# One 512-column value projection in the first head of a hybrid decoder layer

## Chip, cores and metric

The kernel runs on one core of one Trainium2 chip. The metric is the device time of one execution in microseconds (us). The engines are TensorE (PE, with its weight loads listed as PEld), VectorE (DVE), ScalarE (ACT), GpSimd (POOL) and SyncE (SP), whose queue issues nearly all DMAs.

## What is computed

The reference is one decoder layer on 2048 tokens of width 1024, all in float32. Cut to what matters here:

```python
u = rmsnorm(h, norm_mix_w[l])
proj = u @ w_in[l]
hq, hf, hi, hg, att = jnp.split(proj, [...], axis=-1)
...
v_hg = hi.reshape(B, S, HG_HEADS, HG_DV)           # 4 heads of 128 values
o_hg = hgrn2_chunkwise(q_hg, k_hg, v_hg, log_f)    # recurrence, one state per head
o_hg = rmsnorm(o_hg, hg_norm_w[l]) * silu(hg)
...
mix = jnp.concatenate([o_hg, o_att], axis=-1)
h = h + mix @ w_out[l]
```

The recurrence of a head is S_t = diag(f_t) S_{t-1} + k_t v_t^T with the output o_t = S_t^T q_t, where f comes from hf through a sigmoid and k = 1 - f. Beside it stands an attention of 8 query heads over a window of 128 keys. A gated feed-forward part with a short convolution follows, and a last norm.

## The kernel before

**Tiling.** The tokens are worked on in two halves of 1024 (`for hf in range(NH)`). Each half passes through a mixing stage (projections, recurrence, attention), then `out_proj`, `gate_up` and `down`. Every matrix product is made of three: each operand is split into a high part and the rest (`hi`, `lo`; `XH`, `XL`), and hi x hi, hi x lo and lo x hi are added up in PSUM.

**The mixing stage.** It runs over four heads h, and each holds one recurrence head (`hgrn`) and two of the eight query heads (`attend`). Both are generators, and the loop at the end of the listing says in which order their parts are emitted. A head has four units of 128 output columns by 1024 tokens (`unit`, L197): f, hq, q (the attention's query) and g (the gate). A unit is 48 matmuls whose stationary operand is a weight tile and whose moving operand is 512 tokens. The values are made otherwise: in `project_v` the tokens are stationary and the weights move, so that the result has tokens on its partitions. One call makes two heads. For each of 8 tiles of 128 tokens it runs 8 x 3 matmuls of 256 columns (L566 to L568) and two evacuations on ScalarE (L570). It is called in heads 0 and 2.

**The recurrence of a head.** K and Q are made from f and q (L431, L433). Then come a diagonal product `pdiag` (L441), seven levels (`plev`, L467 and L480, with K and Q scaled by VectorE between them), transposes of K (`pkn`, L506), the state updates (`pu`, L513, which read the values), the output products (`po`, L531 and L532, which read the values too), and a norm and transposes back (L540 to L546). K and Q have one buffer each, and the PSUM tiles of this chain two. For the last head the gate unit is emitted ahead of the levels.

**Buffers.** Weights are fetched and split by `prep`: a DMA on SP's queue into a raw ring of three, a cast on ScalarE (L178) and a subtraction on VectorE (L179), into a ring of two pairs `hi`, `lo`. With `slots` set, the pair goes into two of eight slots of 1024 columns instead (tag "m"). These slots are the homes of the mixing results: one for each of the heads' recurrence and attention outputs (`slot`), in use from the head that makes them until `out_proj`. At the end of a half they hold the residual stream, and `finish` writes it out from them (L971). The values have two buffers of one head each (`VB = 2`).

**Order.** A planner fixes the order of each engine's instructions ahead of time: in a simulated timeline an engine takes, of the instructions that are ready, the one that comes first in program order. On the chip each engine then follows its list, and waits where an operand is late. In program order a head's value projection stands behind its levels and its q unit, and ahead of its attention scores (`psc`, L356), its `pkn` and `pu` and its gate unit.

Of the kernel before, what the change touches and what calls it, by code (L numbers as in the profile page):

```python
# [8 lines left out]
F32 = mybir.dt.float32  # L9
# [3 lines left out]
AF = mybir.ActivationFunctionType  # L13
# [4 lines left out]
P = 128  # L18
D = 1024
KT = D // P  # L20
# [3 lines left out]
TT = HALF // P  # L24
NB = HALF // 512
HG = 4
# [12 lines left out]
NEG = -1.0e30  # L39
UT = 7  # L40
RAW = 3
VB = 2


@with_exitstack
def hymba_layer(ctx: ExitStack, tc: tile.TileContext, a: dict, out: bass.AP):
    nc = tc.nc

    def pool(name, bufs=1, space=None, stack=ctx, **kw):
        if space is not None:  # L50
            kw["space"] = space
        return stack.enter_context(tc.tile_pool(name=name, bufs=bufs, **kw))
# [12 lines left out]
    def ps(kind, name):  # L65
        return spaces[kind].tile([P, 512], F32, tag=kind, name=name)
# [98 lines left out]
    def raw4(src):  # L165
        t = wp.tile([P, D], F32, tag="raw", name="raw", bufs=RAW)
        if src is not None:
            nc.sync.dma_start(t, src)
        return t

    def prep(src, slots=False, parts=(slice(0, D),)):

        raw = raw4(None)
        hi, lo = [hp.tile([P, D], F32R, tag="m", name=f"w{t}", bufs=KT) if slots else
                  wp.tile([P, D], F32R, tag=t, name=f"w{t}", bufs=2) for t in ("hi", "lo")]
        for c in parts:
            nc.sync.dma_start(raw[:, c], src[:, c])
            nc.scalar.copy(hi[:, c], raw[:, c])  # L178
            nc.vector.tensor_tensor(lo[:, c], raw[:, c], hi[:, c].bitcast(F32), op=ALU.subtract)  # L179
        return hi, lo  # L180
# [23 lines left out]
    def split(src, w=None, eng=None, dst=None):  # L204

        h, l = dst or new_x()
        if w is None:
            nc.scalar.copy(h, src)
            (eng or nc.vector).tensor_tensor(l, src, h.bitcast(F32), op=ALU.subtract)  # L209
        else:  # L210
            nc.scalar.activation(h, src, AF.Identity, scale=w)
            nc.vector.scalar_tensor_tensor(l, src, w, h.bitcast(F32), op0=ALU.mult, op1=ALU.subtract)
        return h, l
# [338 lines left out]
        nc.vector.tensor_copy(state[:, h], SS[:, TT - 1])  # L552
        yield

    def project_v(hf, pr, X, rs, p):

        v = [p.tile([P, TT, P], F32, tag="v", name="v", bufs=VB) for _ in range(2)]
        parts = [prep(a["w_v"][pr, s]) for s in range(2)]
        for tt in range(TT):
            o = ps("mm", "pvv")  # L560
            t = slice(tt * P, (tt + 1) * P)
            for kt in range(KT):
                hi, lo = parts[kt // 4]
                xh, xl = X[kt]
                c = slice((kt % 4) * 256, (kt % 4 + 1) * 256)
                nc.tensor.matmul(o[:, 0:256], xh[:, t], hi[:, c], start=kt == 0, stop=False)  # L566
                nc.tensor.matmul(o[:, 0:256], xl[:, t], hi[:, c], start=False, stop=False)  # L567
                nc.tensor.matmul(o[:, 0:256], xh[:, t], lo[:, c], start=False, stop=kt == KT - 1)  # L568
            for i in range(2):
                nc.scalar.activation(v[i][:, tt], o[:, i * P:(i + 1) * P], AF.Identity, scale=rs[:, tt:tt + 1])  # L570
        return v

    def split_into(h, l, src, eng=None):
        nc.scalar.copy(h, src)  # L574
# [398 lines left out]
    X, W = [], []  # L973
# [7 lines left out]
    for hf in range(NH):  # L981
        X, kv, invb, rs, f0 = nxt
        with ExitStack() as st:
            p = pool(f"mix{hf}", stack=st, reuse_waits="tile")
            KS, V = att_keys(hf, kv, invb, p)
            mix = [None] * KT
            vs = []
            M, WG = {}, {}
            for h in range(HG):
                hg = hgrn(hf, h, X, invb, vs, WG, mix, p, f0 if h == 0 else None)  # L990
                at = attend(hf, h, X, invb, KS, V, mix, p)
                next(hg)
                if h == HG - 1:
                    next(at)
                    next(hg)
                    for kt in (0, 4, 1, 5, 2, 6):
                        M[kt] = split(mix[kt])
                    next(hg)
                else:
                    next(hg)  # L1000
                    next(at)
                if h % 2 == 0:
                    vs += project_v(hf, h // 2, X, rs, p)
                if h < HG - 1:
                    WG[h] = prep(a["w_g"][h])
                next(at)
                next(hg)
                if h < HG - 1:
                    next(hg)
                next(at)  # L1010
                if h < HG - 1:
                    next(at)
                    next(hg)
                else:
                    next(hg)
                    next(at)
            M[7], M[3] = mix[7], mix[3]
        with ExitStack() as st:
            p = pool(f"ffn{hf}", stack=st, reuse_waits="tile")
            kept, ops, hs, first = out_proj(hf, M, p)  # L1020
            acts = gate_up(hf, ops, hs, first, p)
            nxt = down(hf, kept, acts, p)


def _layout(i):

    import numpy as np

    def cols(w, idx):
        t = w[:, idx].reshape(KT, P, len(idx))  # L1030
        return t.transpose(1, 0, 2).reshape(P, -1)

    x = i["x"][0]
    w_in = i["w_in"][0]
    ar = np.arange
    att0 = 2048
    att = [np.concatenate([att0 + j * HD + ar(HD), att0 + (j + 4) * HD + ar(HD)]) for j in range(4)]
    att += [att0 + 512 + ar(P), att0 + 640 + ar(P)]
    b = i["b_attn"][0]
    rows = [ar(P) + h * P for h in range(4)]  # L1040
    rows += [512 + np.concatenate([j * HD + ar(HD), (j + 4) * HD + ar(HD)]) for j in range(4)]
    w_out = i["w_out"][0][np.concatenate(rows)]
    w_v = np.stack([cols(w_in, 1024 + pr * 256 + ar(256)).reshape(P, 2, D).transpose(1, 0, 2) for pr in range(2)])
    conv = np.concatenate([i["conv_w"][0], i["conv_b"]], 0)
    d = {
        "xT": x.T.reshape(KT, P, S),
        "xP": x[np.where(ar(S) // 512 % 2, ar(S) ^ 31, ar(S))].T.reshape(KT, P, S),
        "norm_mix_w": i["norm_mix_w"][0].reshape(KT, P).T,
        "w_q": np.stack([cols(w_in, h * P + ar(P)) for h in range(4)]),
        "w_f": np.stack([cols(w_in, 512 + h * P + ar(P)) for h in range(4)]),  # L1050
        "w_v": w_v,
        "w_g": np.stack([cols(w_in, 1536 + h * P + ar(P)) for h in range(4)]),
        "w_att": np.stack([cols(w_in, c) for c in att]),
        "b_attn": np.stack([b[c - att0] for c in att], 1),
        "lb_logits": i["lb_logits"].reshape(2, HG, P).transpose(2, 0, 1),
        "hg_norm_w": i["hg_norm_w"].reshape(P, 1),
        "sinks": i["sinks"].reshape(2, 4).T.reshape(1, 8),
        "w_out": np.stack([cols(w_out, t * P + ar(P)) for t in range(KT)]),
        "norm_ffn_w": i["norm_ffn_w"].reshape(KT, P).T,
        "final_norm_w": i["final_norm_w"].reshape(KT, P).T,  # L1060
        "w_gate": np.stack([cols(i["w_gate"][0], t * P + ar(P)) for t in range(FT)]),
        "w_up": np.stack([cols(i["w_up"][0], t * P + ar(P)) for t in range(FT)]),
        "conv": conv.reshape(4, FT, P).transpose(2, 1, 0),
    }

    w = i["w_down"][0].reshape(FT // 2, 2, P, 2, 4, P)
    d["w_down"] = w.transpose(3, 1, 2, 0, 4, 5).reshape(4, P, FT // 2, 512)
    return {k: np.ascontiguousarray(v) for k, v in d.items()}
# [16 lines left out]
```

## Time and profile before

| | |
|---|---|
| median of 3 runs | 2219.83 us (2214.84 to 2221.45) |
| the profiled execution | 2216.09 us, span 2214.4 us |
| granted TensorE clock, mean | 0.996 |
| TensorE busy | 2173.3 us (98%), 11302 matmuls |
| weight loads busy | 1818.8 us (82%) |
| VectorE busy | 1637.8 us (74%) |
| ScalarE busy | 1047.8 us (47%) |
| value projections | 768 matmuls of 256 columns, 64 evacuations |

Busy time is the union of an engine's instructions. Matmuls overlap in the pipeline, so the time from one start to the next, not the duration, is what a matmul costs. The slices of the page cut the span in 40 equal parts; a digit is the busy share in tenths. In the timeline a row gives the start, the length, the engine, the line, the operation, the tiles written and read, the shapes and a count.

### The profile page before, as it was taken

The page shows a single profiled execution, that of the slowest core. Times are in us where ns is not written, and L with a number is a line of the kernel's source. Part 1 is how long each engine was busy: PE and PEld are TensorE (multiplying, and loading weights), DVE is VectorE, ACT ScalarE, POOL GpSimd, SP SyncE. Part 2 cuts the span into 40 slices and gives each one's busy share as a digit, 9 for nine tenths or more (in the row PEclk, how much of TensorE's full clock was granted, in tenths as well). Part 3 has the DMA queues.
Part 4 walks back from the last instruction along what each step waited for, and adds up shares of the span by engine and source line. Part 5 has one row for each costly group of instructions (what it writes and reads, how often), then busy time and mean ns, then how long its engine had stood idle before and what let it go on. Part 6 is the DMA issues. An engine that isn't in the chain of part 4 may idle for free.

```text
span 2214.4 us, 29214 instructions
## 1 busy us (share of the span) xinstructions
PE 2173.3 (98%) x11302; PEld 1818.8 (82%) x11302; DVE 1637.8 (74%) x2458; ACT 1047.8 (47%) x1821; POOL 13.0 (1%) x37
## 2 busy tenths in 40 slices
PE   8999998999999999999999999989999999999997
PEld 6988987778888888888889889878788888888887
DVE  6567568688887888775865666577878888887766
ACT  6445445454444445335725455545544444443353
POOL 2000000000000000000000000000000000000000
PEclk9999999999999999999999999999999999999998
DMA  4111112322333234964631111213232323359643
GB/s 154 39 29 39 29 39 67 107 84 92 113 100 114 88 127 146 372 233 160 201 124 39 29 29 39 67 29 132 66 126 85 124 87 119 96 196 388 223 130 128
DMA packets 89995, 254.15 MB, mean 115 GB/s; under 512 B 11008, under 2 KB 13184, under 8 KB 89856
## 3 DMA queue, kind: packets, MB, share of 16 engines
q1 hardware_dynamic: 87552, 251.17, 33.8%
q8 instruction: 88, 1.44, 0.3%
q10 hardware_dynamic: 2304, 1.12, 0.2%
q14 instruction: 51, 0.42, 0.1%
HBM read 195.10 MB, written 57.15 MB: 114 GB/s over the span
## 4 chain that ended last, share of the span: by engine, by line
PE 94%; DVE 3%; ACT 1%; DMA 1%; issue 0%; SPq 0%; DVEq 0%; ACTq 0%
PE X L697 7%; PE X L698 7%; PE X L699 7%; PE pop L197 6%; PE hq L197 4%; PE f L197 4%; PE q L197 4%; PE g L197 4%; PE pdx L879 4%; PE pdx L880 4%; PE pdx L881 4%; PE Y L697 4%; PE Y L699 4%; PE Y L698 4%; PE pdy L880 3%; PE pdy L879 3%
## 5 line engine op out<-in xcount | busy, mean ns | idle before, releaser
L574 ACT CAST whi<-raw 128x1024 fp32r<-128x1024 f32 x88 | 92.7, 1053 | 109.3 <-PE X L698 66.8
L698 PE MATMUL X<-T,whi 128*128 128x512 f32 x352 | 137.3, 390 | 0.0
L697 PE MATMUL X<-T,whi 128*128 128x512 f32 x352 | 137.0, 389 | 0.0
L699 PE MATMUL X<-T,wlo 128*128 128x512 f32 x352 | 136.9, 389 | 0.0
L763 DVE SCALAR_TENSOR_TENSOR y<-ga,cw,y 128x1024 f32<-128x1024 f32 x88 | 112.5, 1279 | 28.1 <-ACT y L761 28.1
L703 ACT COPY u<-X 128x512 f32<-128x512 f32 x88 | 51.6, 587 | 121.6 <-PE X L699 121.3
L575 DVE TENSOR_TENSOR wlo<-raw,whi 128x1024 fp32r<-128x1024 f32 x88 | 107.2, 1218 | 0.0
L575 DVE TENSOR_TENSOR xld<-raw,xhd 128x1024 fp32r<-128x1024 f32 x72 | 80.8, 1132 | 18.9 <-ACT xhd L574 18.6
L178 ACT CAST whi<-raw 128x1024 fp32r<-128x1024 f32 (+2 forms) x61 | 63.0, 1035 | 62.0 <-PE hq L197 12.4
L574 ACT CAST xhd<-raw 128x1024 fp32r<-128x1024 f32 x72 | 69.6, 978 | 43.2 <-DMA raw<-act0T 14.7
L197 PE MATMUL pop<-XL,whi 128*128 128x512 f32 x256 | 84.8, 395 | 3.5 <-DVE XL L209 3.5
L197 PE MATMUL pop<-XH,wlo 128*128 128x512 f32 x256 | 83.8, 393 | 0.8 <-DVE wlo L179 0.8
L197 PE MATMUL pop<-XH,whi 128*128 128x512 f32 x256 | 84.1, 400 | 0.2
L179 DVE TENSOR_TENSOR wlo<-raw,whi 128x1024 fp32r<-128x1024 f32 (+2 forms) x61 | 73.2, 1204 | 13.2 <-ACT whi L178 13.2
L697 PEld LDWEIGHTS X<-T,whi 128*128 128x128 f32 x352 | 66.1, 188 | 14.0 <-ACT u L703 0.3
L699 PEld LDWEIGHTS X<-T,wlo 128*128 128x128 f32 x352 | 66.1, 188 | 13.9 <-issue 0.2
L698 PEld LDWEIGHTS X<-T,whi 128*128 128x128 f32 x352 | 66.1, 188 | 13.9 <-issue 0.2
L879 PE MATMUL pdx<-xhd,hid 128*128 128x512 f32 x192 | 74.5, 391 | 1.0 <-ACT hid L574 1.0
L880 PE MATMUL pdx<-xld,hid 128*128 128x512 f32 x192 | 74.8, 390 | 0.0
L697 PE MATMUL X<-T,Sh 128*128 128x512 f32 x176 | 68.7, 390 | 5.3 <-ACT s L703 5.3
L881 PE MATMUL pdx<-xhd,lod 128*128 128x512 f32 x192 | 73.7, 389 | 0.0
L567 PE MATMUL pvv<-whi,XL 128*128 128x256 f32 x256 | 73.1, 287 | 0.0
(359 smaller groups left out, 6530.8 us busy)
## 6 DMA issues: line engine op xcount, KB each, us to landing
wr<-in_w_down SPq DMA_DIRECT2D x90, 512.0 KB, 5.6
raw<-in_w_gate SPq DMA_DIRECT2D x44, 512.0 KB, 3.7
raw<-in_w_up SPq DMA_DIRECT2D x44, 512.0 KB, 3.6
raw<-act0T SPq DMA_DIRECT2D x20, 512.0 KB, 5.9
raw<-act1T SPq DMA_DIRECT2D x20, 512.0 KB, 5.6
act0B<-y SPq DMA_DIRECT2D x33, 256.0 KB, 2.3
act1B<-y SPq DMA_DIRECT2D x33, 256.0 KB, 2.5
raw<-in_w_out SPq DMA_DIRECT2D x16, 512.0 KB, 4.0
```

What stands on the lines that cost most here:

```text
L179: nc.vector.tensor_tensor(lo[:, c], raw[:, c], hi[:, c].bitcast(F32), op=ALU.subtract)
L197: nc.tensor.matmul(o[b], w, x[:, bs], start=f, stop=l)
L567: nc.tensor.matmul(o[:, 0:256], xl[:, t], hi[:, c], start=False, stop=False)
L574: nc.scalar.copy(h, src)
L575: (eng or nc.vector).tensor_tensor(l, src, h.bitcast(F32), op=ALU.subtract)
L697: nc.tensor.matmul(o, wh[:, ws], xh, start=i == 0 and not more, stop=False, skip_group_check=more)
L698: nc.tensor.matmul(o, wh[:, ws], xl, start=False, stop=False, skip_group_check=more)
L699: nc.tensor.matmul(o, wl[:, ws], xh, start=False, stop=i == 3, skip_group_check=more)
L763: nc.vector.scalar_tensor_tensor(y, g[:, w:w + HALF], C.cw[:, ft, w:w + 1], y, op0=ALU.mult, op1=ALU.add)
L879: nc.tensor.matmul(o, wh[:, i, c], ah[:, i, cols], start=f, stop=False, skip_group_check=more)
L880: nc.tensor.matmul(o, wh[:, i, c], al[:, i, cols], start=False, stop=False, skip_group_check=more)
L881: nc.tensor.matmul(o, wl[:, i, c], ah[:, i, cols], start=False, stop=l, skip_group_check=more)
```

## The change

The values of all four heads come from one call, in head 0. A matmul now moves 512 columns, and the 8 x 3 matmuls of a token tile fill a whole PSUM bank. The weights are four pieces of two contraction tiles each. The first goes into the ring, the three others into six of the result slots, which are free in head 0 apart from two. One evacuation per token tile writes all four heads. The values have one buffer for the whole half.

```diff
-VB = 2
...
-    def project_v(hf, pr, X, rs, p):
-
-        v = [p.tile([P, TT, P], F32, tag="v", name="v", bufs=VB) for _ in range(2)]
-        parts = [prep(a["w_v"][pr, s]) for s in range(2)]
+    def project_v(X, rs, p):
+
+        v = p.tile([P, HG, TT, P], F32, tag="v", name="v", bufs=1)
+        parts = [prep(a["w_v"][s], s > 0) for s in range(4)]
         for tt in range(TT):
             o = ps("mm", "pvv")
             t = slice(tt * P, (tt + 1) * P)
             for kt in range(KT):
-                hi, lo = parts[kt // 4]
+                hi, lo = parts[kt // 2]
                 xh, xl = X[kt]
-                c = slice((kt % 4) * 256, (kt % 4 + 1) * 256)
-                nc.tensor.matmul(o[:, 0:256], xh[:, t], hi[:, c], start=kt == 0, stop=False)
-                nc.tensor.matmul(o[:, 0:256], xl[:, t], hi[:, c], start=False, stop=False)
-                nc.tensor.matmul(o[:, 0:256], xh[:, t], lo[:, c], start=False, stop=kt == KT - 1)
-            for i in range(2):
-                nc.scalar.activation(v[i][:, tt], o[:, i * P:(i + 1) * P], AF.Identity, scale=rs[:, tt:tt + 1])
-        return v
+                c = slice(kt % 2 * 512, (kt % 2 + 1) * 512)
+                nc.tensor.matmul(o, xh[:, t], hi[:, c], start=kt == 0, stop=False)
+                nc.tensor.matmul(o, xl[:, t], hi[:, c], start=False, stop=False)
+                nc.tensor.matmul(o, xh[:, t], lo[:, c], start=False, stop=kt == KT - 1)
+            nc.scalar.activation(v[:, :, tt], o.rearrange("p (h d) -> p h d", h=HG), AF.Identity, scale=rs[:, tt:tt + 1])
+        return [v[:, h] for h in range(HG)]
...
-                if h % 2 == 0:
-                    vs += project_v(hf, h // 2, X, rs, p)
+                if h == 0:
+                    vs += project_v(X, rs, p)
...
-    w_v = np.stack([cols(w_in, 1024 + pr * 256 + ar(256)).reshape(P, 2, D).transpose(1, 0, 2) for pr in range(2)])
+    w_v = cols(w_in, 1024 + ar(512)).reshape(P, 4, D).transpose(1, 0, 2)
```

## The prediction

> **What bounds the kernel now.** I read the page first, for the engines and the slices.
>
> ```profile
> span 2214.4 us, 29214 instructions
> ...
> PE 2173.3 (98%) x11302; PEld 1818.8 (82%) x11302; DVE 1637.8 (74%) x2458; ACT 1047.8 (47%) x1821; POOL 13.0 (1%) x37
> ...
> PE   8999998999999999999999999989999999999997
> ...
> PEclk9999999999999999999999999999999999999998
> ```
>
> TensorE is busy 98% of the span at a full clock nearly everywhere, so work taken off TensorE shortens the kernel wherever nothing else is late. The changed work lies in the mixing stage: about 33 to 393 us for the first half of the tokens, 1130 to 1488 us for the second. Next I asked for windows, all instructions in stretches of 10 us (columns: PE busy, PEld, DVE, ACT, POOL, granted clock, DMA).
>
> ```profile
> 80.00:90.00 10.00, 10.00 (x87) 10.00 (x86) 3.36 (x6) 2.57 (x9) 0.00 (x0) 1.00 0.00 0
> 90.00:100.00 10.00, 10.00 (x117) 9.62 (x116) 2.59 (x4) 4.03 (x10) 0.00 (x0) 1.00 0.01 2
> ...
> 220.00:230.00 10.00, 10.00 (x71) 8.03 (x70) 0.00 (x0) 1.80 (x9) 0.00 (x0) 1.00 0.01 2
> ...
> 310.00:320.00 10.00, 10.00 (x75) 8.44 (x74) 1.85 (x3) 2.23 (x10) 0.00 (x0) 1.00 0.19 55
> ...
> 350.00:360.00 10.00, 6.46 (x34) 4.73 (x34) 10.00 (x18) 3.71 (x8) 0.00 (x0) 0.97 0.35 105
> 360.00:370.00 10.00, 9.32 (x34) 7.89 (x35) 7.37 (x17) 7.48 (x35) 0.00 (x0) 0.69 0.01 2
> ```
>
> ```profile
> 340.00:400.00 60.00, 53.39 (x376) 45.06 (x375) 43.42 (x88) 25.97 (x80) 0.00 (x0) 0.94 0.13 38
> 1436.00:1496.00 60.00, 52.47 (x383) 43.75 (x382) 42.63 (x88) 26.14 (x80) 0.00 (x0) 1.00 0.13 37
> ```
>
> Two regimes are to be seen. Up to 340 us TensorE has no idle time and VectorE waits for it; between 350 and 360 us VectorE is full and TensorE waits. This is the tail of head 3, where TensorE has run out of units that don't need head 3's recurrence. The two tails cost 60 - 53.39 = 6.6 us and 60 - 52.47 = 7.5 us of idle TensorE. The waits of that stretch name the recurrence:
>
> ```profile
> PE plev L467 <- ACT G L465: 1.9, 1, 1.9
> PE pop L197 <- DVE XL L209: 1.8, 1, 1.8
> ```
>
> Last came the timeline of TensorE (start, length, instruction), for where the recurrence stands beside the units.
>
> ```profile
> 156.33 0.83 PE L441 MATMUL pdiag<-hg,K 128*128 128x128 f32 x6
> 229.70 0.61 PE L197 MATMUL q<-XH,wlo 128*128 128x512 f32 x2
> 234.69 0.39 PE L532 MATMUL po<-SS,Q 128*128 128x128 f32 x2
> 246.44 1.73 PE L441 MATMUL pdiag<-hg,K 128*128 128x128 f32 x14
> 306.15 0.39 PE L531 MATMUL po<-v,ST 128*128 128x128 f32 x2
> 324.50 0.39 PE L532 MATMUL po<-SS,Q 128*128 128x128 f32 x2
> 335.62 0.62 PE L197 MATMUL g<-XH,wlo 128*128 128x512 f32 x2
> 344.31 1.95 PE L441 MATMUL pdiag<-hg,K 128*128 128x128 f32 x16
> 386.91 0.38 PE L531 MATMUL po<-v,ST 128*128 128x128 f32 x2
> 392.32 0.39 PE L532 MATMUL po<-SS,Q 128*128 128x128 f32 x2
> ```
>
> A head's recurrence opens with its diagonal product (L441) and closes with its output products (L531, L532): 156.3 to 235.1 for head 1, 246.4 to 324.9 for head 2, 344.3 to 392.7 for head 3. The next head's Q has one buffer and must wait for the close. So the recurrence of the four heads is a second, serial chain, and after its last close come only units whose number is fixed. The half ends when the later of the two is through: TensorE's units or this chain.
>
> **The change, part by part.** *Matmuls.* Starts, not durations, tell the cost, since durations overlap.
>
> ```profile
> 91.04 0.28 PE L568 MATMUL pvv<-wlo,XH 128*128 128x256 f32 x1
> ...
> 94.63 0.28 PE L568 MATMUL pvv<-wlo,XH 128*128 128x256 f32 x1
> ```
>
> ```profile
> 703.02 0.39 PE L697 MATMUL X<-T,whi 128*128 128x512 f32 x1
> ...
> 707.78 0.39 PE L697 MATMUL X<-T,Sh 128*128 128x512 f32 x1
> ```
>
> Thirty steps of 256 columns take 3.59 us, 0.1197 us each; twenty-one steps of 512 columns, with new stationary weights at each, take 4.76 us, 0.2267 us each. The change removes 4 stages x 192 = 768 of the first (91.9 us) and adds 2 x 192 = 384 of the second (87.1 us): **-4.8 us**, 2.4 per half. The Trainium skill, in "TensorE: Matmul & The Clock Gate", section "Back-to-back issue gap", gives N/2.4 + 2.5 ns, hence by estimate 109.2 and 215.8 ns, and the sum would be only -1.0 us; the trace's steps are 10 to 11 ns longer, so I go by the rows.
>
> *Evacuations.* 64 copies of 128 columns become 32 of 512.
>
> ```profile
> L570 ACT ACTIVATE v<-pvv,y 128x128 f32<-128x128 f32 x32 | 10.0, 363 | 20.9 <-PE pvv L568 20.8
> L333 ACT ACTIVATE att<-att,bq 128x512 f32<-128x512 f32 x8 | 5.5, 717 | 1.7 <-DVE att L331 1.7
> ...
> L703 ACT COPY u<-X 128x512 f32<-128x512 f32 x88 | 51.6, 587 | 121.6 <-PE X L699 121.3
> ```
>
> Bounded by the last two rows the new one takes 587 to 717 ns: 18.8 to 22.9 us in place of 64 x 363 = 23.2. ScalarE is 47% busy and a token tile now lasts 24 x 0.2267 = 5.4 us against 0.7 to evacuate it; four PSUM banks cover that. Nothing.
>
> *Weight pieces.* Four per half before and after, but two move from head 2 to head 0 with their DMAs on SP's queue, two casts and two subtractions (here over 18 such).
>
> ```profile
> L179 DVE TENSOR_TENSOR wlo<-raw,whi 128x1024 fp32r<-128x1024 f32 x18 | 21.9, 1216 | 4.5 <-ACT whi L178 4.5
> ...
> 1166.30:1195.00 28.70, 24.39 (x192) 23.35 (x192) 4.38 (x14) 1.00 0.06 19
> ...
> 1128.01 4.55 SPq L971 DMA_DIRECT2D out<-h  x8
> ```
>
> That is 2.4 us of VectorE in head 0, hidden by the long projection. In the second half three pieces need six result slots, whose last contents leave by 1132.6 us; the projection lay between 1166.3 and 1195.0 (the row of its own instructions above), which leaves 34 us. In return the second ring slot is free for the next weights. If a piece came late, planned work of later heads would fill in; up to 2 us, taken as nothing.
>
> *The move.* In head 0 the projection grows from 192 x 0.1197 = 23.0 us to 192 x 0.2267 = 43.5, and in head 2 the 23.0 us vanish. Program order puts the scores of a head and its recurrence updates behind the projection, so in head 0 VectorE, at 3.36 and 2.59 of 10 us above, stays that idle for 20.5 us more, and everything through the start of head 2's recurrence comes 20.5 us later. TensorE loses nothing by that. But behind head 2's q unit, which ended at 230.2, TensorE had 336.1 - 230.2 = 105.9 us of work before it ran dry, and now has 82.9, while the chain has the same steps: 324.9 - 230.2 = 94.7 us to the close of head 2, then 67.8 us to the close of head 3. If the chain kept its pace, both closes would come 20.5 us late in each half: the upper bound. If it gained all of it, the half would gain 2.4 us.
>
> It will gain much. The output products of head 2 took 306.15 to 324.9 = 18.7 us, in four batches with q units between; those of head 3, with no units left to put between, took 386.9 to 392.7 = 5.8. With the units used up by 82.9 us, head 2 closes in the same way: **12.9 us back**. Head 2's scores no longer stand behind a projection, and can use stretches such as 220 to 230 us, where VectorE did nothing; some of head 3's attention moves ahead of the tail too. Bounds are 0 and the 10 us of that stretch; I take 3, nearer to 0, since the rest of this stage has VectorE full for short spells only. So per half 20.5 - 12.9 - 3 = 4.6 us later, **about +9 us** in all; the matmul gain is inside this, since the chain sets the end. The profiled execution took 2216.1 us (span 2214.4), 3.7 under the median of 2219.8: 2225 in its terms, 2229 beside the median.
>
> **The rivals.** *The chain follows TensorE* (not slower): VectorE had 10 and 8.2 idle us at 220 and 310; if it uses 10 of these rather than 3 in each half, the chain keeps step with the shorter TensorE work (20.5 - 12.9 - 10 = -2.4 per half), and the -4.8 us show: 2215. It decides at the point where head 3's diagonal product comes no more than 8.2 us behind the end of the last g unit, as 344.3 behind 336.1 now. For it: VectorE waited for TensorE all the way to 340. Against: full VectorE from 350.
>
> *The tail shrinks as well*: attention of head 3 done ahead of the tail takes half of the 14.1 idle us with it: -4.8 - 7 = -12, 2208.
>
> *No pace is gained*: the planner keeps head 2's batches apart, and both closes come 20.5 us late: +41 us, 2261. Against it are the 5.8 us of head 3. The granted clock fell to 0.69 behind the idle stretch in the rows above. The same page of the Trainium skill, section "Why this matters for your kernels", warns of TensorE gaps over about 3 us, after which the clock halves; the 0.69 agrees, and this would add to a longer tail.
>
> *The matmuls don't get cheaper*: at 2 x 0.1197 a step the gain is nothing; the 512-column row with new weights at each step speaks against it.
>
> **How the numbers follow.** The forecast, 2229 with 2226 to 2235 as its own range (VectorE's share of the catch-up between 4.3 and 0 us per half), gets 0.40; the chain following, 2213 to 2226, 0.29; the shrinking tail 0.19; no pace gained, with what lies between it and the forecast, 0.12. About 0.3%, 6.7 us, is what a measurement of this kernel can tell from no change. So faster 0.19, same 0.29, slower 0.52. The range runs from 2207, which cuts off a part of the shrinking tail, to 2248, which cuts off most of the last case.
>
> **What would show it.** Right: 512-column steps of 0.227 us in one stage of some 49 us per half; head 1's diagonal product near 177 us; head 2's output products within 10 us; head 3's close at about 397 and the idle time of 340 to 400 grown by some 7 us. Wrong: head 3's close before 392, or VectorE busy over 60% while the projection runs; steps of 0.24 would undo the first term, and a TensorE wait on a weight piece the third.

## The result, and the profile after

The changed kernel took 2232.87 us (median of 4 runs, 2228.82 to 2235.33) beside 2220.22 us (2214.84 to 2221.45) for the kernel before: a ratio of 1.0058 with a 95% interval of 1.0047 to 1.007, so slower by over 0.3%. The profiled execution took 2228.82 us, its span 12.7 us longer than before.

The page of the changed kernel, in the parts shown of before:

```profile
span 2227.1 us, 28404 instructions
...
PE 2173.5 (98%) x10918; PEld 1802.1 (81%) x10918; DVE 1634.4 (73%) x2458; ACT 1036.7 (47%) x1771; POOL 14.1 (1%) x37
...
PE   8999997999999999999999999989999999999997
```

There are 384 matmuls fewer, but TensorE's busy time is the same, and the seventh slice (334 to 390 us) has gone from 8 to 7: there the loss shows. The timeline of TensorE in the changed kernel (start, length, instruction) gives the same marks as before; its line numbers are one or two lower:

```profile
82.98 0.39 PE L565 MATMUL pvv<-whi,XH 128*128 128x512 f32 x1
...
85.70 0.39 PE L565 MATMUL pvv<-whi,XH 128*128 128x512 f32 x1
...
176.42 0.38 PE L440 MATMUL pdiag<-hg,K 128*128 128x128 f32 x2
...
271.91 0.38 PE L440 MATMUL pdiag<-hg,K 128*128 128x128 f32 x2
...
335.50 0.27 PE L530 MATMUL po<-v,ST 128*128 128x128 f32 x1
...
343.45 0.39 PE L531 MATMUL po<-SS,Q 128*128 128x128 f32 x2
...
354.81 0.46 PE L440 MATMUL pdiag<-hg,K 128*128 128x128 f32 x1
...
397.86 0.39 PE L531 MATMUL po<-SS,Q 128*128 128x128 f32 x2
...
1500.68 0.39 PE L531 MATMUL po<-SS,Q 128*128 128x128 f32 x2
```

Twelve steps of 512 columns take 85.70 - 82.98 = 2.72 us, 0.227 each. The recurrence of head 1 opens 20.1 us later than before, that of head 2 25.5, that of head 3 10.5, and head 3 closes 5.5 us later. In the second half the close stands at 1500.7, where it stood in the kernel before at

```profile
1487.74 0.39 PE L532 MATMUL po<-SS,Q 128*128 128x128 f32 x2
```

which is 12.9 us: the whole loss is in by then, 5.5 us from the first half of the tokens and 7.4 from the second. The windows over the two tails of the changed kernel (PE busy, PEld, DVE, ACT, POOL, granted clock, DMA, GB/s) show where:

```profile
340.00:400.00 60.00, 47.04 (x330) 38.03 (x329) 39.33 (x84) 20.93 (x73) 0.00 (x0) 0.91 0.06 19
...
340.00:410.00 70.00, 57.04 (x377) 46.13 (x376) 44.27 (x95) 22.18 (x75) 0.00 (x0) 0.93 0.05 16
1446.00:1516.00 70.00, 58.16 (x381) 47.15 (x381) 46.33 (x99) 20.71 (x61) 0.00 (x0) 0.93 0.08 24
```

TensorE is idle for 12.96 and 11.84 us in these tails, where it was idle for 6.6 and 7.5, and for 2.2 us more just ahead of the last window. Over the whole span its idle time is 2227.1 - 2173.5 = 53.6 us, before 2214.4 - 2173.3 = 41.1: 12.5 us more. The clock is the other part. Smaller windows, first of the changed kernel, then of the kernel before:

```profile
342.00:344.00 2.00, 0.71 (x4) 0.52 (x4) 1.08 (x3) 1.99 (x12) 0.00 (x0) 1.00 0.00 0
344.00:346.00 2.00, 1.08 (x5) 1.08 (x6) 2.00 (x4) 0.24 (x2) 0.00 (x0) 0.69 0.01 4
346.00:348.00 2.00, 0.89 (x5) 0.48 (x3) 2.00 (x4) 0.00 (x0) 0.00 (x0) 0.50 0.00 0
...
352.00:354.00 2.00, 1.86 (x12) 1.49 (x9) 1.51 (x4) 1.70 (x10) 0.00 (x0) 0.50 0.00 0
354.00:356.00 2.00, 1.95 (x12) 1.41 (x11) 2.00 (x4) 0.00 (x0) 0.00 (x0) 0.75 0.04 8
...
1446.00:1451.00 5.00, 2.65 (x12) 2.09 (x12) 5.00 (x9) 0.98 (x7) 0.00 (x0) 0.63 0.01 2
1451.00:1456.00 5.00, 4.55 (x33) 3.62 (x34) 4.60 (x20) 3.10 (x16) 0.00 (x0) 0.50 0.01 3
1456.00:1461.00 5.00, 4.58 (x30) 4.02 (x30) 4.60 (x8) 1.95 (x4) 0.00 (x0) 0.85 0.00 0
```

```profile
358.00:360.00 2.00, 0.74 (x7) 0.54 (x5) 2.00 (x6) 0.98 (x3) 0.00 (x0) 0.85 0.00 0
360.00:362.00 2.00, 1.32 (x6) 1.35 (x7) 2.00 (x3) 0.58 (x1) 0.00 (x0) 0.50 0.00 0
```

Before, TensorE ran at half clock once, for some 7 us; in the second tail the clock stayed at 1.00. Now it runs at half clock in both tails for some 10 us each. TensorE's busy time stayed the same although 4.8 us of matmuls went, so by estimate some 5 us of it are the slower clock's. Each window's busy time times (1 - clock) gives nearly the same: 4.0 and 3.9 us in the two tails now, 2.8 us before. So the span grew by 12.5 us of idle time and about 5 us of clock, less 4.8 us of matmuls: 12.7 us.

### The profile page after: what moved, and what is told of

Its sections match the earlier page's. It is cut to its first block, busy times and chain, and to the rows that moved or that the text cites. A ratio compares the mean times of both kernels' runs of the same rounds, so it can differ in the third digit from the quotient of the medians.

```text
span 2227.1 us, 28404 instructions
## 1 busy us (share of the span) xinstructions
PE 2173.5 (98%) x10918; PEld 1802.1 (81%) x10918; DVE 1634.4 (73%) x2458; ACT 1036.7 (47%) x1771; POOL 14.1 (1%) x37
## 4 chain that ended last, share of the span: by engine, by line
PE 92%; DVE 5%; ACT 2%; DMA 1%; issue 0%; SPq 0%; DVEq 0%; ACTq 0%
PE X L695 7%; PE X L696 7%; PE X L697 7%; PE pop L196 6%; PE q L196 4%; PE g L196 4%; PE hq L196 4%; PE f L196 4%; PE pdx L877 4%; PE pdx L878 4%; PE pdx L879 4%; PE Y L695 4%; PE Y L697 4%; PE Y L696 4%; PE pdy L878 3%; PE pdy L877 3%
## 5 line engine op out<-in xcount | busy, mean ns | idle before, releaser
L177 ACT CAST whi<-raw 128x1024 fp32r<-128x1024 f32 (+2 forms) x61 | 62.8, 1035 | 78.8 <-PE hq L196 18.2
L695 PE MATMUL Z<-B,whi 128*128 128x512 f32 x176 | 68.9, 392 | 0.0
```

The lines of the kernel that those rows point to most:

```text
L695: nc.tensor.matmul(o, wh[:, ws], xh, start=i == 0 and not more, stop=False, skip_group_check=more)
```

## The experiments

The question was what makes the late recurrence cost so much. The theories bear these letters in the expectations: **A**, VectorE's idle time beside the long projection comes back as work in the tail; **B**, units of fixed length are missing beside the late part of the chain of recurrences; **C**, Q's single buffer holds the next head; **D**, the output products wait for their PSUM banks; **E**, the order of scores and state updates paces head 2; **F**, heads 2 and 3 are held by the amount of work on VectorE. Further runs tried single parts of the change. Ratios are to the kernel before, with 95% intervals from 5 rounds.

### Width and place apart

Each 512-column matmul of the changed kernel becomes two of 256, so that the place of the change stays and its width goes; the cut shows the first of the three products.

```diff
+                for i in range(2):
+                    oi, ci = o[:, i*256:(i+1)*256], slice(c.start + i*256, c.start + (i+1)*256)
-                nc.tensor.matmul(o, xh[:, t], hi[:, c], ...)
+                    nc.tensor.matmul(oi, xh[:, t], hi[:, ci], ...)
```

> The changed kernel with each 512-column value matmul made as two of 256 columns: the place, the buffers and the evacuations stay, only the width is undone. If all that follows head 0 is shifted by the longer projection, the matmul term of 4.8 us passes to the end in full: 2237.5, ratio 1.008 to the kernel before. If the end is set by the chain of the recurrences and the width is hidden: as the changed kernel, 1.0058. If the matmuls' fixed cost were 2.5 ns: 1.006.

It took 2237.68 us, 1.0075 [1.0063, 1.0088]. The instructions of the projection alone, in this run and then in the changed kernel:

```profile
72.60:124.40 51.80, 47.63 (x384) 46.30 (x383) 4.83 (x7) 1.00 0.15 45
```

```profile
71.30:120.80 49.50, 45.27 (x192) 35.44 (x192) 4.81 (x7) 1.00 0.15 46
```

From 130 to 340 us TensorE, VectorE and ScalarE run the same instructions in the same order in both runs, so little but the width differs. The stage is 2.3 us longer per half, 4.6 in all. The medians differ by 4.8 us, the ratios by 0.0017 or 3.8 us, and the two intervals overlap a little. So **the width brings about its 4.8 us, and the place costs about 17** (0.0075 x 2220).

### VectorE's work beside the projection (A)

The scores of head 0 are emitted ahead of the projection, in the changed kernel; as a control the same in heads 0 and 2 of the kernel before.

```diff
                 if h == 0:
+                    next(at)
                     vs += project_v(X, rs, p)
-                next(at)
+                if h:
+                    next(at)
```

> The changed kernel with head 0's attention scores emitted ahead of the long projection, so that VectorE has that work during it. Theory A (the loss is VectorE's idle time during the projection): the tails come back by up to 6 us each, 2220, ratio 1.000, and VectorE is busy over 50% during the projection. Theory B (the loss is the missing TensorE work beside the recurrence of head 2 and later): ratio 1.004 to 1.006, the tails as long as in the changed kernel.

> The kernel before with the scores of heads 0 and 2 emitted ahead of their projections, a control for the run scores_first. Theory A: VectorE was idle for some 10 us in each projection, so faster by 0.2 to 0.5%. Theory B: within 0.2%.

They took 2235.43 us, 1.0065 [1.0053, 1.0078], and 2223.5 us, 1.0015 [1.0006, 1.0024]. The windows of the first, over the projection and over the tail:

```profile
71.80:124.90 53.10, 53.10 (x305) 44.70 (x304) 29.30 (x49) 30.11 (x74) 0.00 (x0) 1.00 0.14 42
340.00:402.00 62.00, 48.80 (x335) 40.00 (x334) 39.47 (x84) 21.68 (x77) 0.00 (x0) 0.89 0.06 18
```

VectorE was now busy 29.30 of 53.1 us (in the changed kernel 18.82 of 49.5), and the tail still had 62 - 48.80 = 13.2 idle us. From 180 to 340 us the order on all three engines is that of the changed kernel. **A falls** as far as this edit tries it: moving head 0's scores beside the projection gives nothing back, and in the control neither.

### What a projection costs in head 2 (and C)

In the kernel before, head 2's projection is left out, and heads 2 and 3 read the values of heads 0 and 1. A second version adds another buffer for Q.

```diff
-                if h % 2 == 0:
+                if h == 0:
                     vs += project_v(hf, h // 2, X, rs, p)
+                    vs += vs[:2]
```
```diff
-        Q = p.tile([P, HALF], F32, tag="Q", name="Q", bufs=1)
+        Q = p.tile([P, HALF], F32, tag="Q", name="Q", bufs=2)
```

> The kernel before without head 2's projections (2 x 192 matmuls of 256 columns, 46 us of TensorE, left out; heads 2 and 3 read the values of heads 0 and 1). If TensorE set the end throughout, 46 us go: 2174, ratio 0.979. If the serial chain of the recurrences sets the end once that work is gone: about 20.5 - 6 = 14.5 us per half, 2191, ratio 0.987, with the tails' idle time of TensorE grown by some 8 us each.

> The run drop2 (the kernel before without head 2's projections; heads 2 and 3 read the values of heads 0 and 1), with two buffers for Q instead of one. Theory C (Q's one buffer strings the heads together: head 3's first level waits for head 2's output products): the first level of head 3 moves ahead of them, and up to 10 us per half come back: 2174 to 2182, ratio 0.979 to 0.983. Theory D (the two PSUM banks of the recurrence string them together): no change, 0.988.

They took 2193.83 us, 0.988 [0.9867, 0.9894], and 2191.72 us, 0.9868 [0.9855, 0.9882]. The two projections left out are 2 x 192 x 0.1197 = 46.0 us of TensorE, with their weight pieces and evacuations; only 0.012 x 2220 = 26.6 us came back. The rest is mostly idle time of TensorE in the tails, as the window over the first one shows:

```profile
322.00:382.00 60.00, 45.70 (x332) 37.08 (x332) 38.94 (x81) 21.62 (x77) 0.00 (x0) 0.94 0.07 19
```

That is 14.3 idle us, where the tail had 6.6; from 1400 to 1480 us it is 14.0. Over the span the idle time is 57.0 us in place of 41.1, and the slower clock takes some 6 us more. **So 19 us of a projection in head 2 cost nothing: without it the chain of recurrences still takes that time.** From this run to the changed kernel, which has all values again, with 2 x 20.5 = 41 us more in head 0, the time grows by 2232.87 - 2193.83 = 39.0 us: **in head 0 nearly nothing is hidden**. The 19 us are the price of the place, near the 17 of the first experiment. The timeline of the first version:

```profile
326.14 0.39 PE L532 MATMUL po<-SS,Q 128*128 128x128 f32 x2
337.50 1.16 PE L441 MATMUL pdiag<-hg,K 128*128 128x128 f32 x8 [0.75 <-DVE hg L546]
...
380.59 0.39 PE L532 MATMUL po<-SS,Q 128*128 128x128 f32 x2
```

From the close of head 2 to the start of head 3 to its close are 11.36 and 43.09 us, in the changed kernel 11.36 and 43.05: the same chain, 17.3 us later. Head 0's hq unit began at 48.95 us in this run and at 45.87 in the changed kernel, so against that start the chain is 20.4 us later, the length that head 0 gained. With two buffers for Q head 3 closes at 377.83, and the time falls by 2.1 us, with overlapping intervals. Of these 2.8 us at the close 2.5 stand already at head 0's hq unit (46.45 against 48.95), and head 3's diagonal product still comes behind head 2's close (333.98 against 324.96). **C brings nothing that can be seen here.**

### Links of the chain (D, E, B)

Three edits of the changed kernel: the output products in the PSUM banks of the units; head 2's scores behind its state updates; and the gate units of heads 0 to 2 each emitted one head later, to put 48 matmuls per half beside the late chain (with one silu in place of sigmoid and product).

```diff
-        po = [ps("hg", "po") for _ in range(NB)]
+        po = [ps("mm", "po") for _ in range(NB)]
```
```diff
+                if h == 2:
+                    next(hg)
                 next(at)
-                next(hg)
+                if h != 2:
+                    next(hg)
```
```diff
-            gate()
+            late[h] = q
...
+                    if h:
+                        late_gate(h - 1, X, invb, WG, p)
```

> The changed kernel with the output products of the recurrence in the PSUM banks of the units in place of the recurrence's own two. Theory D (the output products hold both banks until the norm is through, 10.8 us past their end, and head 3's diagonal product and levels wait for a bank): head 3's diagonal product moves ahead of 344 us and 5 to 10 us per half come back, 2213 to 2223, ratio 0.997 to 1.001. Theory C (Q's one buffer): head 3's first level still needs the output products to be through, at most 2 us per half, 1.004 to 1.006.

> The changed kernel with head 2's attention scores emitted behind its state updates, so that VectorE serves the levels first. Theory E (head 2's levels are slowed by its own attention on VectorE, 38 us from the first to the last against 34 before): they take some 34 us again and 2 to 4 us per half come back, ratio 1.002 to 1.004. If the work is only moved into the tail: 1.006 or more.

> The changed kernel with the gate units of heads 0, 1 and 2 each held back by one head (the normed recurrence output goes into its slot first and is gated there later, with one silu in place of sigmoid and product): 10.9 us of TensorE per half leave head 0 and come beside the last recurrence; as many vector operations as before. Theory B (the loss is TensorE work that no longer stands beside the late recurrences): the tails fill and 4 to 11 us per half come back: 2211 to 2225, ratio 0.996 to 1.002. Theory F (the chain and VectorE of heads 2 and 3 close when they close, wherever the units stand): 1.005 to 1.008.

The first took 2247.43 us, 1.0128 [1.0113, 1.0144]. Its timeline, at the end of head 3's q unit, the start of head 3 and its close:

```profile
339.15 0.62 PE L196 MATMUL q<-XH,wlo 128*128 128x512 f32 x2
...
342.56 1.95 PE L440 MATMUL pdiag<-hg,K 128*128 128x128 f32 x16
...
402.69 0.39 PE L531 MATMUL po<-SS,Q 128*128 128x128 f32 x2
```

Head 3 starts 12 us earlier than in the changed kernel, as D has it, but the q unit, which ended there at 312, now ends at 339.8, and the close is later. TensorE was now idle for 4.4 us between 200 and 280 us and for 4.3 between 280 and 340, where the changed kernel has none. The edit costs more than it tests, so what **D** is worth **stays open**. The second took 2234.47 us, 1.0063 [1.005, 1.0076], and head 2's levels took as long as in the changed kernel. But the edit did not do what it was meant to: from 70 to 340 us TensorE, VectorE and ScalarE run the same instructions in the same order as in the changed kernel, since the planner came to the same lists. **E stays untested.** The third took 2245.25 us, 1.0111 [1.0095, 1.0128]. Its window over the tail:

```profile
340.00:420.00 80.00, 63.24 (x399) 52.68 (x400) 48.89 (x107) 26.11 (x88) 0.00 (x0) 0.87 0.07 21
```

TensorE was idle for 16.8 us there, not less, head 3 closed at 406.7, and head 1 started at 176.0, no earlier. The two gate units of this stretch ran from 300.2 to 330.5 us, ahead of the tail and not in it. So the run shows that this order is slower; **B**, units beside the late chain, **was not brought about** and stays open.

### The weight pieces, and head 1 ahead

In the kernel before, head 0's two pieces are put in result slots, as three of the four are in the change. And in both kernels the f and hq units of the next head are emitted ahead of this head's gate.

```diff
-        parts = [prep(a["w_v"][pr, s]) for s in range(2)]
+        parts = [prep(a["w_v"][pr, s], pr == 0) for s in range(2)]
```
```diff
+                    ahead = hgrn(hf, h + 1, X, invb, vs, WG, mix, p)
+                    next(ahead)
                 next(hg)
```

> The kernel before with both weight pieces of head 0's projection in result slots, as in the changed kernel, width and place left alone. Theory of the place (the move between the heads is the whole loss): 0.999 to 1.001. If keeping the pieces in result slots holds up weights or results: slower by 0.3% or more.

> The changed kernel with the f and hq units of the next head emitted ahead of this head's gate unit, so that the next recurrence can open as soon as this one closes (in the changed kernel head 1's diagonal product came 21 us behind head 0's last output product, right behind the hq unit). Theory B (the serial chain is late for want of an early start and of units beside it): head 1's diagonal product moves from 176 to about 160 us, the tails shrink, 5 to 15 us per half come back: 2203 to 2223, ratio 0.992 to 1.001. Theory F (heads 2 and 3 are bound by the amount of work on VectorE): the start moves but the close of head 3 does not, 1.004 to 1.007.

> The same order in the kernel before. Theory B: the tails' 6.6 and 7.5 us of idle TensorE mostly go, 2207 to 2215, ratio 0.994 to 0.998. Theory F: 0.999 to 1.003.

The slots alone took 2229.23 us, 1.0036 [1.0024, 1.0049], slower, as the second half of the expectation has it. The timeline of ScalarE and the waits of TensorE (total, times, longest) show a part of it:

```profile
72.33 1.99 ACT L178 CAST whi<-raw 128x1024 fp32r<-128x1024 f32 x2 [0.53 <-PE q L197]
```

```profile
PE pvv L568 <- DVE wlo L179: 1.1, 1, 1.1
```

Both pieces were cast only at the end of the q unit, and the projection waited for them: 1.1 us for this subtraction and 0.7 for a cast. That the order in which slots are handed out is the reason is argued, and where the rest of the 8 us arose isn't shown. In the changed kernel the first piece lies in the ring, and no wait of TensorE stands between 60 and 125 us: this wait is no part of its loss.

The two with the next head's units ahead took 2235.63 us, 1.0072 [1.0059, 1.0086], and 2225.86 us, 1.0025 [1.0015, 1.0035]. In the changed kernel so edited hq of head 1 ended early, but its diagonal product came later (187.0, not 176.4):

```profile
155.59 0.62 PE L196 MATMUL hq<-XH,wlo 128*128 128x512 f32 x2
...
187.01 0.54 PE L440 MATMUL pdiag<-hg,K 128*128 128x128 f32 x3
```

So what the expectation rested on did not come about, and the run says only that this order brings nothing.

### Subtractions off VectorE

The six subtractions that split the mixing results ahead of head 3 go to GpSimd.

```diff
-                        M[kt] = split(mix[kt])
+                        M[kt] = split(mix[kt], eng=nc.gpsimd)
```

> The changed kernel with the subtractions of the six operand splits ahead of head 3's levels on GpSimd, 7 us of VectorE per half. Theory F (VectorE's work): up to 7 us per half come back, ratio 1.000 to 1.003. Theory B (the chain's steps one behind the other): at most 2 us per half, 1.004 to 1.006, or slower where GpSimd takes longer for the same.

It took 2235.09 us, 1.0067 [1.0054, 1.0081]: nothing gained, so F isn't borne out, though the longer subtractions may have used up a gain. The timeline of GpSimd:

```profile
323.56 2.40 POOL L208 TENSOR_TENSOR XL<-hg,XH 128x1024 fp32r<-128x1024 f32 x1 [311.51 <-ACT XH L207]
...
331.11 3.36 POOL L208 TENSOR_TENSOR XL<-att,XH 128x1024 fp32r<-128x1024 f32 x1
```

No version with all of the work was faster than the kernel before.

## Why the prediction was right, and where its parts were not

**Steps.** 0.227 us was forecast and measured, in a stage of 49.5 us, and in the first experiment the narrow matmuls cost 4.6 us by the stage and 4.8 by the medians. By the Trainium skill, "TensorE: Matmul & The Clock Gate", section "Back-to-back issue gap", which gives its formula for isolated matmuls, they would by estimate cost 1.0 us more; the measured stage decides for the rows.

**Evacuations and weight pieces.** Rightly nothing. The new evacuation lies between its bounds of 587 and 717 ns, as the group of the changed kernel shows:

```profile
L568 ACT ACTIVATE v<-pvv,y 128x512 f32<-128x512 f32 x16 | 11.0, 687 | 52.9 <-PE pvv L567 52.9
```

The reason given for the slots was that their contents leave in time. The run with both pieces in slots shows another condition, that the first piece is ready when the projection opens; in the changed kernel it is.

**The move.** The direction and the mechanism hold: the chain of recurrences sets the end, the longer head 0 shifts it, it gains much of it back, and the loss shows as idle TensorE at the close. Head 1 opened at 176.4 (forecast 177), head 3 closed at 397.9 (397), and the idle time of 340 to 400 us grew by 13.0 - 6.6 = 6.4 (7). The close came 5.5 us late in the first half and 7.4 more in the second, against 4.6 each; in all 12.7 us against 9. One reading was wrong: TensorE did not run dry at 336.1 us, with the end of the last g unit. It went on with units of `out_proj`, and its first idle stretch began at 348.6 (now at 341.7).

**Inside, the terms were mis-sized, and that they nearly cancel is luck.** The output products of head 2 took 335.5 to 343.8 = 8.3 us in place of 18.7, so 10.4 of the 12.9 came. But head 2 opened 25.5 us late and not 20.5: head 1 took 2.0 us longer from opening to close (80.8 in place of 78.8), and from its close to head 2's opening it was 14.7 us in place of 11.4. And head 2's levels ran longer, 38.0 us in place of 33.8, as their first and last rows of the changed kernel and of the one before show:

```profile
277.14 1.07 PE L466 MATMUL plev<-Q,G 128*128 128x128 f32 x8
...
314.91 0.22 PE L479 MATMUL plev<-Q,K 128*64 128x64 f32 x1
```

```profile
250.50 1.07 PE L467 MATMUL plev<-Q,G 128*128 128x128 f32 x8
...
283.16 1.15 PE L480 MATMUL plev<-Q,K 128*64 128x64 f32 x16
```

So head 2 closed 19 us late, not 7.6. The term of 3 us, work of head 3 that moves ahead of the tail, was in fact 8.4 + 5.0 = 13.4: from head 2's close to head 3's opening it is 11 us, where it was 19.4, and from there to the close 43.4, where it was 48.4. Part of the work that moved is seen in the timeline of VectorE, by the last of four such splits in the changed kernel and the first of four in the one before:

```profile
324.74 1.22 DVE L208 TENSOR_TENSOR XL<-att,XH 128x1024 fp32r<-128x1024 f32 x1
```

```profile
328.47 1.22 DVE L209 TENSOR_TENSOR XL<-hg,XH 128x1024 fp32r<-128x1024 f32 x1
```

These splits stood behind head 2's close (324.9), and now stand ahead of it (343.8). That they and the scores of head 3 lengthen head 2's levels in return is argued from their order, not shown: the run with the subtractions on GpSimd gave nothing back.

**The clock** was named only as something that would worsen a longer tail. By the estimate above it is about 5 us beside 12.5 us of idle time, and had no term in the sum. Nor was the reading right that the 0.69 agrees with a warning of gaps over 3 us: in the kernel before, the fall came at about 359.4 us (0.85 over 358 to 360) behind idle stretches of 0.4 and 1.2 us, and the longest one there lasted 1.95.

**The rivals.** "No pace is gained" would have been +41 us; the pace gained is 41 - 13. "The chain follows TensorE" asked for head 3's diagonal product within 8.2 us behind the end of the last g unit; it came 27.6 us behind (354.8 against 327.2). "The tail shrinks as well" fails too, as the idle time grew. "The matmuls don't get cheaper" is refuted by the steps and by the first experiment.

**Open** is what paces heads 2 and 3 between 250 and 400 us as a whole. Of the edits, Q's second buffer, the units of the next head ahead and GpSimd gave nothing; the score order and the late units did not come about as meant; the PSUM banks couldn't be tried without moving the units. One link the trace of the changed kernel shows, in VectorE's timeline between head 2's close and head 3's opening:

```profile
346.23 0.16 DVE L151 TENSOR_SCALAR ms<-ss 128x8 f32<-128x8 f32 x1
...
351.98 1.29 DVE L539 TENSOR_TENSOR on<-po,y 128x512 f32<-128x512 f32 x2
...
354.05 0.70 DVE L545 SCALAR_TENSOR_TENSOR hg<-pot,hgw,hg 128x512 f32<-128x512 f32 x1
```

Head 2's norm lasts from 346.2 to 353.3 us, with attention work on VectorE in between. Head 3's diagonal product has had its K since 323.7 us and its q for longer, yet starts at 354.81, when VectorE has read the first of head 2's two transposed blocks out of PSUM (354.75); its second part starts at 356.60, the second block is read at 356.54. That fits the wait for a bank that D names, for this one link. How much time it costs in the end no run shows. Shown is the price: a TensorE microsecond costs nearly its full length in head 0 (39 of 41), and 26.6/46 = 0.58 of it in head 2.

## What to carry to other kernels

A TensorE stage has a price by its place: beside a serial chain that lasts longer than the units left for it, part of it is free, so fewer and wider matmuls can lose when they are moved away from that chain. Test width and place apart, by running the new place with the old width. And look in a chain's tail for short idle stretches of TensorE, since they can cost clock as well: here about 5 us beside 12.5 us of idle time. And look in the trace whether an edit of the program's order changed the engines' order at all, before its time is read as an answer.

## What the runs showed of the hardware

**Half clock without a long gap.** Ahead of the fall at about 345 us TensorE's idle stretches in the changed kernel, and the longest behind it, were these:

```profile
343.13 0.49 PE L530 MATMUL po<-v,ST 128*128 128x128 f32 x2 [1.47 <-ACT on L532]
...
344.92 1.97 PE L391 MATMUL ppt<-ident,sc 128*128 128x128 f32 x8 [1.08 <-DVE sc L364]
348.85 1.48 PE L402 MATMUL poT<-po,V 128*64 128x128 f32 x7 [1.97 <-DVE y L154]
```

None is as long as 2 us, and the clock was at 0.50 for 10 us all the same, to 354 and beyond, though TensorE was busy for 1.86 of the 2 us from 352 on. The Trainium skill, "TensorE: Matmul & The Clock Gate", section "Why this matters for your kernels", asks for no gap over about 3 us; here the clock fell behind gaps of 1.5 and 1.1 us, and in the second half behind one of 2.6. What sets it off isn't settled: a stretch at 384 to 388 us with less work, and with two gaps of 1.5 us, left the clock at 1.00.

```profile
384.00:388.00 4.00, 1.33 (x30) 1.11 (x23) 2.44 (x4) 1.30 (x3) 0.00 (x0) 1.00 0.00 0
```

**Subtraction on GpSimd.** The same 128x1024 subtraction took 2.40 to 3.36 us there and 1.22 us on VectorE.

**Weight loads.** With 256 columns the loads were busy for 46.3 of 51.8 us of the projection, with 512 for 35.4 of 49.5. Whether the loads set the narrow step wasn't tried.
